# Gate pairs of a two-group trunk layer: the two sums that are rounded first are made directly behind the merges, and the last two merged tiles are split in written order

## The chip, the cores and the metric

The kernel runs on one core of one Trainium2 chip. The metric is the device time of one execution in microseconds (us). The kernel before the change takes 1002.07 us, the median of 3 runs (1001.85 to 1002.22).

## What is computed

One layer of a hybrid backbone is applied to two groups of tokens: a context group of 128 tokens and a denoising group of 512 tokens, 640 tokens together, model width 1024, all in float32. The part that matters here is the gated merge of four token mixers and what stands on both sides of it:

```
    h = rmsnorm(x, lw['norm1_g']) * (1.0 + sc1) + sh1
    mix, kh, vh, s_f, s_b = token_mixers(h, lw, ...)        # ends in the lines below
    x = x + g1 * mix
    h = rmsnorm(x, lw['norm2_g']) * (1.0 + sc2) + sh2
    x = x + g2 * conv_ffn(h, lw['w_up'], ...)
...
    g_a, g_b, g_c, g_d = jnp.split(jax.nn.sigmoid(h @ lw['w_gate'] + lw['b_gate']), N_BRANCH, axis=-1)
    merged = (g_a * (y_a @ lw['w_br_a']) + g_b * (y_b @ lw['w_br_b'])
              + g_c * (y_c @ lw['w_br_c']) + g_d * (y_d @ lw['w_br_d']))
    return merged @ lw['w_o'], kh, vh, s_f, s_b
```

Each of the four gates is a 1024 x 1024 product with `h`, each `w_br_*` a 256 x 1024 product with a mixer's output.

## The kernel before, in words

**Arithmetic.** Every float32 operand of a matmul is split into a high part, rounded by a copy on ScalarE (`oact(..., AF.Copy)`), and a low part, the difference, taken on VectorE (`low`, L1131). A product is three matmuls per 128 rows: high x high, high x low, low x high.

**Gate pairs.** Most of the gate products are done in pairs: output tile n and output tile n+4 of one branch together, by a 2 x 2 block scheme with seven products instead of eight (`gprod`, products 1 to 7, 12 matmuls each; `bprod` does the same for the branch's own weights, 3 matmuls each). There are GPAIR = 14 pairs, (0,2), (0,3) and then four pairs for each of the branches 1, 2 and 3. Pairs 0, 2, 6 and 10 are the first of their branch (`new`). One pair is 105 matmuls.

**What a pair prepares for the next.** For pair n = p+1, pair p makes three weight units from the loaded blocks `r[n]` (names `raw` and `G` in the profile): unit A (`g_a`: high and low of the first block row), unit B (`g_b`: high and low of two sums S0, S1 that `g_sums` makes; they lie in the tile named `D`), and unit C (`g_c`). `g_sums` makes four VectorE additions: S0 and S1 into `D`, then two more in place in `G`/`raw` that unit C and the Z unit (tile `S`) use. A unit's tile is called `w`, every fourth one `B`.

**What a pair computes.** ScalarE and VectorE carry partial results between PSUM banks: `gb` (twice per pair on ScalarE, from bank b1, tile `m`), `ga`, `y`. VectorE then subtracts `gb` from bank b2 (the row `gb<-m,gb`), after which product 3 goes on accumulating in b2: TensorE's product 3 therefore waits for that subtraction. The merges of pair p-1 (`g_merges`, L1213: gate times branch product, added to the merged tiles `MG`) are done in pair p, behind its first product.

**The order of the work.** A scheduler orders each engine's instructions, except those issued through `ovec`, `oact` and `opool` while `fixed[0]` is True: these keep their written order among themselves (`Ordered`, L141 to L151; so they all carry L151). TensorE's order is the scheduler's. `fixed[0]` is set in `g_all` for the pairs.

**Behind the pairs.** `m_split(i)` (L1223) makes high and low of a quarter of the merged tiles, into the tiles `E`, `D`, `B`, `A` for i = 0 to 3. Splits 0 and 1 stand in the last pair; splits 2 and 3 stand behind the merges of the last pair, when `fixed[0]` is False already. `wo_tile` (from L1359, matmuls at L1381) multiplies the merged tiles with w_o in the order E, D, B, A: in its first half all five token blocks accumulate in one bank `m` and four halves of the two banks `g`. VectorE then reads the results out (`wt`, L1391) and adds them to x (L1393). In the last quarter (A) the third and fourth `g` group wait for the first `wt` row that reads a `g` bank. Beside it `up_early` (L1502 to L1547) splits the first weights of the next layer part: loads into `XH` and `XL` (L1508), rounds (L1512), takes the low part (L1513), adds (L1532, L1536) and stores to `upd` (L1519, L1542, L1546). The w_o weights are rounded at L323 and L324. `norm2` (from L1403) normalises each token block and transposes it (L1425).

Of the kernel before, what the change touches and what calls it, by code (L numbers as in the profile page):

```python
# [13 lines left out]
ALU = mybir.AluOpType  # L14
# [56 lines left out]
def tile_step(ctx: ExitStack, tc: tile.TileContext, a: dict, outs: list, dbg=None):  # L71
# [54 lines left out]
    def nm(s):  # L126
        cnt[0] += 1
        return f"{s}_{cnt[0]}"

    def region(tag, shape, dt=F32):  # L130
        return big.tile(shape, dt, tag=tag, name=nm(tag))
# [7 lines left out]
    fixed, boot = [False], [True]  # L139
# [17 lines left out]
    ovec, opool, oact = Ordered(nc.vector), Ordered(nc.gpsimd), Ordered(nc.scalar).activation  # L157
# [802 lines left out]
    for s in SECTIONS:  # L960
        for n in range(2):
            if s in TOK:
                plain(lambda s=s, n=n: rows(a["w_tok"][TOK.index(s), n], 4, 256),
                      lambda w, s=s, n=n: tok_tile(s, n, w))
            else:
                plain(lambda s=s, n=n: feat(a["w_in"][OFF[s] // P + n], dma=s in LOWD),
                      lambda w, s=s, n=n: in_tile(s, n, w))
# [23 lines left out]
    GPAIR = len(PAIRS)  # L991
# [44 lines left out]
    gx, gw = {}, {}  # L1036
# [59 lines left out]
    def y_split():  # L1096
        bi = gx["bi"]
        c, y = gx["C"], R["y" + BR[bi]]
        src = [gx["Y"][:, i * HC:j * HC] for i, j in ((0, 2), (3, 4), (2, 3))]
        dst = [[c[:, h, 0:2].rearrange("p i t -> p (i t)"), c[:, h, 2], y[:, h, 0, HC:T]] for h in range(2)]  # L1100
        for o, x in zip(dst[0][:2], src):
            oact(o, x, AF.Copy)
        lows = [(l, x, h) for h, l, x in zip(dst[0], dst[1], src)]
        return lows[:2], lows[2]
# [26 lines left out]
    def low(w, x, h):  # L1131
        ovec.tensor_tensor(w, x, h.bitcast(F32), ALU.subtract)

    def g_a(p_, r):
        w = gw[p_, "A"] = gunit(p_, 0)
        oact(w[:, 0], r[0], AF.Copy)
        low(w[:, 1], r[0], w[:, 0])

    def g_sums(p_, r):

        s = gw[p_, "S"] = gx["S"] if p_ else region("G", [P, 2, 5, P])
        b21, (b22, b12) = r[0][:, 1], (r[1][:, 0], r[1][:, 1])
        ovec.tensor_tensor(s[:, 0], r[0][:, 0], b12, ALU.add)
        ovec.tensor_tensor(s[:, 1], s[:, 0], b22, ALU.add)
        ovec.tensor_tensor(b12, b12, b22, ALU.add)
        ovec.tensor_tensor(b21, s[:, 1], b21, ALU.add)

    def g_b(p_):
        s = gw[p_, "S"]
        b = gw[p_, "B"] = gunit(p_, 1)  # L1150
        oact(b[:, 0], s, AF.Copy)
        low(b[:, 1], s, b[:, 0])
# [21 lines left out]
    def gprod(o, p_, i, first):  # L1174
        u, n = GPROD[i]
        w = gw[p_, u]
        xh_, xl_ = gx["x"][i]
        for k in range(4):
            for j, (h, x) in enumerate(((0, xh_), (0, xl_), (1, xh_))):
                mm(o, w[:, h, n, k, :], x[:, k, :], start=(first and k == 0 and j == 0),  # L1180
                   stop=(k == 3 and j == 2), skip_group_check=True)
            tick(0.44)
# [9 lines left out]
    def g_merge(p_, i, pb):  # L1192
        bi, n = gp_id(p_)
        n += 4 * i
        gt = gw[p_, "gt", i]
        mg = merged[n // 4][:, n % 4, :]
        ovec.tensor_tensor(c2(gt if bi else mg), pb, c2(gt), ALU.mult)
        if not bi:
            return
        ovec.tensor_tensor(mg, mg, gt, ALU.add)  # L1200

    def g_sig(p_, i, o, x):
        bi, n = gp_id(p_)
        gc = C_BG + GI[BR[bi]] * 8 + n + 4 * i
        oact(o, x, AF.Sigmoid, bias=p1[:, gc:gc + 1])
# [7 lines left out]
    def g_merges(q):  # L1213
        ps, b2, y = gw[q, "ps"], gw[q, "b2"], gw[q, "y"]
        g_merge(q, 0, ps[:, :, 0:HC])
        ovec.tensor_tensor(y[:, 0:HC], b2, y[:, 0:HC], ALU.subtract)
        g_merge(q, 1, c2(y))
        if PAIRS[q] in ((0, 3), (1, 3)):
            n_, t, y = ("yb", "E", ybd) if PAIRS[q][0] == 0 else ("yc", "A", ycd)
            R[n_] = region(t, [P, 2, 2, T], F32R)  # L1220
            pool.dma_start(R[n_], y)

    def m_split(i):  # L1223
        n = 2 * MHN[i]
        w = mh[MHN[i]] = region(MHT[i], [P, 2, 2, T], F32R)
        x = merged[n // 4][:, n % 4:n % 4 + 2, :]
        oact(w[:, 0], x, AF.Copy)
        ovec.tensor_tensor(w[:, 1], x, w[:, 0].bitcast(F32), ALU.subtract)

    def g_pair(p_, r):  # L1230
        n, q = p_ + 1, p_ - 1
        inner, nx = p_ < GPAIR, n < GPAIR
        if not inner:
            g_sig(q, 1, gw[q, "gt", 1], gw[q, "gt", 1])
            g_close(q)
            g_merges(q)
            return
        bi, n0 = gp_id(p_)
        new = n0 == (NPL if bi == 0 else 0)
        if new:  # L1240
            gx["bi"] = bi
        if n0 == (NPL if bi == 0 else 0) + 1 and bi < 3:
            y_load(bi + 1)
        b1, b3 = pm()[:, 0:HC], pm()[:, 0:HC]
        ga = gw[p_, "gt", 0] = gp.tile([P, T], F32, tag="gt", name=nm("ga"))
        gb = gw[p_, "gt", 1] = gp.tile([P, T], F32, tag="gt", name=nm("gb"))
        g_zl(p_, r[p_])
        gprod(b1, p_, 1, True)
        if q >= 0:
            g_sig(q, 1, gw[q, "gt", 1], gw[q, "gt", 1])  # L1250
        oact(b3 if q >= 0 else ga[:, 0:HC], b1, AF.Copy)
        if q >= 0:
            g_close(q)
        ps = gw[p_, "ps"] = pg()
        p1_, p3_ = ps[:, 1, 0:HC], ps[:, 0, 0:HC]
        bprod(p1_, p_, 1, True)
        oact(p3_, p1_, AF.Copy)
        if q >= 0:
            g_merges(q)
        if nx:  # L1260
            g_a(n, r[n])
        lows, x3 = y_split() if new else ([], None)
        gprod(b3, p_, 2, q < 0)
        if q < 0:
            g_split(3, gx["t3"][0])
            ovec.tensor_tensor(ga[:, 0:HC], b3, ga[:, 0:HC], ALU.add)
        g_sig(p_, 0, ga[:, 0:HC], b3 if q >= 0 else ga[:, 0:HC])
        for x in lows:
            low(*x)
        gprod(b1, p_, 6, False)  # L1270
        oact(gb[:, 0:HC], b1, AF.Copy)
        bprod(p3_, p_, 2, False)
        b2 = pm()[:, 0:HC]
        gprod(b2, p_, 5, True)
        if nx:
            g_sums(n, r[n])
            if not new:
                g_b(n)
        gprod(b1, p_, 7, False)
        oact(gb[:, HC:T], b1, AF.Copy)  # L1280
        y = gw[p_, "y"] = gp.tile([P, T], F32, tag="gt", name=nm("y"))
        c2_ = gw[p_, "b2"] = pm()[:, 0:HC]
        bprod(p1_, p_, 6, False)
        oact(y[:, 0:HC], p1_, AF.Copy)
        bprod(c2_, p_, 5, True)
        ovec.tensor_tensor(gb[:, HC:T], b2, gb[:, HC:T], ALU.subtract)
        if new:
            g_b(n)
        if nx:
            late = g_c(n, r[n])  # L1290
            if not new:
                for x in late:
                    low(*x)
            if n + 1 < GPAIR:
                r[n + 1] = gp_load(n + 1)
        else:
            m_split(0)
            m_split(1)
        gprod(b1, p_, 4, False)
        g_sig(p_, 0, ga[:, HC:T], b1)  # L1300
        bprod(p1_, p_, 7, False)
        oact(y[:, HC:T], p1_, AF.Copy)
        if new:
            oact(x3[2], x3[1], AF.Copy)
            low(*x3)
        if nx:
            g_zh(n, r[n])
        gprod(b2, p_, 3, False)
        if n0 == (NPL if bi == 0 else 0) + 1 and bi < 3:
            y_sums()  # L1310
        ovec.tensor_tensor(y[:, HC:T], c2_, y[:, HC:T], ALU.subtract)
        ovec.tensor_tensor(gb[:, 0:HC], b2, gb[:, 0:HC], ALU.subtract)
        if new:
            for x in late:
                low(*x)

    def g_first(r):
        drain(lambda: "ada39" in R)
        g_a(0, r[0])
        g_sums(0, r[0])  # L1320
        g_b(0)
        for x in g_c(0, r[0]):
            low(*x)
        g_zh(0, r[0])
        return r

    def g_all(r):
        drain(lambda: "gx3" in R)
        r[1] = gp_load(1)
        gx["C"] = region("C", [P, 2, 3, HC], F32R)  # L1330
        fixed[0] = True
        sums_ = down_sums()
        for p_ in range(GPAIR + 1):
            for _ in range(4 if p_ else 0):
                next(sums_, None)
            if p_ == GPAIR:
                fixed[0] = False
                for j in range(GATES + 1, GATES + 3):
                    ld[j] = units[j][0]()
                    rd[j] = units[j][1](ld[j])  # L1340
            g_pair(p_, r)
        m_split(2)
        m_split(3)

    PROD = {1: ("A", 0, 2), 2: ("A", 1, 3), 5: ("B", 0, 2), 6: ("B", 1, 3), 7: ("B", 4, 4),
            4: ("C", 0, 2), 3: ("C", 1, 3)}
# [1093 lines left out]
    for i in range(3):  # L2440
        sec, n = SECTIONS[i // 2], i % 2
# [109 lines left out]
```

## Time and profile before

| | |
|---|---|
| median of 3 runs | 1002.07 us (1001.85 to 1002.22) |
| the profiled execution | 1002.13 us |
| its span (first to last instruction) | 1000.4 us |
| granted TensorE clock | 0.998 |
| TensorE busy | 987.6 us (99% of the span) |
| VectorE / ScalarE busy | 861.4 us / 584.5 us |
| gate pairs | 309.7 to 525.3 us of the span |
| first half of w_o | 525.3 to 555 us |

A row of a timeline gives start, duration, engine, line, operation, tile written <- tiles read, shape and count; in brackets the idle time of the engine just before and what ended it. PE is TensorE's matmul, PEld its weight load, DVE VectorE, ACT ScalarE, POOL GpSimd, SPq SyncE's DMA queue. Back to back, the start of one VectorE instruction follows the start of the one before it a little sooner than the printed duration says, so costs in a queue are read from starts. Rows of the chain that ended last give start, duration and what.

### The profile page before, as it was taken

How to read it: one execution, taken by the hardware profiler on the slowest of the kernel's cores; microseconds unless marked ns; L12 is line 12 of the kernel's file. 1: busy time of each engine (PE TensorE's matmuls, PEld its weight loads, DVE VectorE, ACT ScalarE, POOL GpSimd, SP SyncE). 2: the span in 40 equal slices, each digit the busy share in tenths (PEclk: the TensorE clock that was granted, in tenths of full speed). 3: DMA queues.
4: the chain of work that ended last, by engine and by line, in shares of the span. 5: the costliest groups of instructions: out<-in, count | busy, mean ns of one | idle time of the engine just before them, and what ended most of it. 6: DMA issues, size and time to landing. Idle time of an engine off the chain costs nothing.

```text
span 1000.4 us, 18963 instructions
## 1 busy us (share of the span) xinstructions
PE 987.6 (99%) x7467; PEld 936.1 (94%) x7467; DVE 861.4 (86%) x1411; ACT 584.5 (58%) x1009; POOL 170.2 (17%) x227
## 2 busy tenths in 40 slices
PE   8999999999999999999999999999999999999997
PEld 6899999999999999999998799999999999888886
DVE  6678899878677989899879978999999998999796
ACT  6652343445555565555656476777777777756672
POOL 1000020313110223233010021222222222100004
PEclk9999999999999999999999999999999999999999
DMA  9874343498475999899448785766666666976742
GB/s 351 333 255 152 126 139 120 132 254 254 106 216 185 305 240 237 285 252 297 111 159 322 298 317 160 216 160 173 177 168 164 177 170 193 369 259 221 280 127 105
DMA packets 71016, 214.16 MB, mean 214 GB/s; under 512 B 9744, under 2 KB 24880, under 8 KB 68240
## 3 DMA queue, kind: packets, MB, share of 16 engines
q1 hardware_dynamic: 43968, 151.22, 43.1%
q0 software_dynamic: 26960, 61.75, 26.7%
q8 instruction: 58, 0.95, 0.4%
q14 instruction: 30, 0.25, 0.1%
HBM read 168.62 MB, written 48.51 MB: 217 GB/s over the span
## 4 chain that ended last, share of the span: by engine, by line
PE 91%; DVE 3%; DMA 3%; issue 1%; POOL 1%; SPq 0%; ACT 0%; POOLq 0%; ACTq 0%
PE g L1609 21%; PE m L1180 17%; PE g L375 16%; PE m L2081 9%; PE m L1609 5%; PE g L2081 4%; PE g L1189 3%; PE m L1381 3%; PE g L948 2%; PE m L1189 1%; PE m L539 1%; PE m L1604 1%; DMA B<-in_w_ada_dram 1%; DMA S<-in_w_ada_dram 1%; PE g L151 1%
## 5 line engine op out<-in xcount | busy, mean ns | idle before, releaser
L375 PE MATMUL g<-XH,w 128*128 128x320 f32 x704 | 169.4, 316 | 0.0
L375 PEld LDWEIGHTS g<-XH,w 128*128 128x128 f32 x704 | 120.3, 188 | 2.5 <-issue 1.2
L375 PE MATMUL g<-XL,w 128*128 128x320 f32 x352 | 108.7, 309 | 0.0
L1180 PE MATMUL m<-XH,w 128*128 128x320 f32 x336 | 79.8, 309 | 0.0
L375 PEld LDWEIGHTS g<-XL,w 128*128 128x128 f32 x352 | 66.3, 188 | 0.0
L2081 PE MATMUL m<-w,XH 128*128 128x512 f32 x246 | 58.5, 390 | 0.0
L1180 PEld LDWEIGHTS m<-XH,w 128*128 128x128 f32 x336 | 57.6, 188 | 0.0
L2081 PEld LDWEIGHTS m<-w,XH 128*128 128x128 f32 x246 | 46.1, 188 | 9.6
L1180 PE MATMUL m<-XL,w 128*128 128x320 f32 x168 | 51.9, 309 | 0.0
L151 ACT ACTIVATE w<-raw 128x640 fp32r<-128x640 f32 (+3 forms) x53 | 49.6, 952 | 3.2 <-PE g L375 2.0
L151 DVE TENSOR_TENSOR w<-raw,w 128x640 fp32r<-128x640 f32 (+3 forms) x43 | 44.0, 1040 | 2.6 <-ACT w L151 2.6
L151 POOL DMA_DIRECT2D wsum<-in_w_dn_dram x36 | 37.4, 1256 | 43.3 <-issue 39.4
L1180 PE MATMUL m<-X,w 128*128 128x320 f32 x264 | 42.6, 309 | 0.0
L151 DVE SCALAR_TENSOR_TENSOR X<-MG,p2t,X 128x641 f32<-128x641 f32 x44 | 38.9, 884 | 1.0 <-ACT X L151 0.2
L1180 PEld LDWEIGHTS m<-X,w 128*128 128x128 f32 x264 | 39.7, 188 | 0.0
L151 DVE SCALAR_TENSOR_TENSOR X<-X,p2t,X 128x641 f32<-128x641 f32 x44 | 38.9, 884 | 0.9
L1609 PE MATMUL g<-XL,w 128*128 128x320 f32 x240 | 38.7, 310 | 0.0
L1609 PE MATMUL g<-XL,C 128*128 128x320 f32 x240 | 38.3, 309 | 0.0
L1609 PEld LDWEIGHTS g<-XL,w 128*128 128x128 f32 x240 | 36.0, 188 | 0.6 <-ACT MG L151 0.3
L1609 PEld LDWEIGHTS g<-XL,C 128*128 128x128 f32 x240 | 36.0, 188 | 0.0
L1180 PEld LDWEIGHTS m<-XL,w 128*128 128x128 f32 x168 | 31.5, 188 | 0.0
L336 ACT ACTIVATE w<-raw 128x1024 fp32r<-128x1024 f32 (+1 forms) x22 | 24.3, 1102 | 12.3 <-PE m L948 8.2
(612 smaller groups left out, 2840.8 us busy)
## 6 DMA issues: line engine op xcount, KB each, us to landing
wsum<-in_w_dn_dram POOLq DMA_DIRECT2D x30, 512.0 KB, 11.0
raw<-in_w_up_dram SPq DMA_DIRECT2D x30, 512.0 KB, 5.2
raw<-in_w_gp_dram SPq DMA_DIRECT2D x21, 640.0 KB, 5.8
raw<-in_w_in_dram SPq DMA_DIRECT2D x19, 512.0 KB, 4.2
H<-in_w_adt_dram SPq DMA_DIRECT2D x19, 512.0 KB, 4.0
raw<-wsum SPq DMA_DIRECT2D x12, 512.0 KB, 5.5
actx<-X POOLq DMA_DIRECT2D x22, 256.0 KB, 4.8
wsum<-wsum POOLq DMA_DIRECT2D x10, 512.0 KB, 10.6
```

What stands on the lines that cost most here:

```text
L151: r = f(*args, **kw)
L336: high = lambda: act(w[:, 0], raw, AF.Copy)
L375: mm(o, w[:, h, k0 + k, :], r(k)[:, s], start=(k == 0 and i == 0), stop=(k == kt - 1 and i == 2))
L539: mm(m[W * g:W * g + W, (i - s0) * W:(i - s0 + 1) * W], lhs, rhs, start=True, stop=True, tile_position=(64 * par, W * g))
L948: mm(o, x(kx)[:, ts], w[:, h, k, :], start=(kx == 0 and i == 0), stop=(kx == 7 and i == 2))
L1180: mm(o, w[:, h, n, k, :], x[:, k, :], start=(first and k == 0 and j == 0), stop=(k == 3 and j == 2), skip_group_check=True)
L1189: mm(o, w[:, h, n, 4, :], x[l], start=(first and j == 0), stop=(j == 2), skip_group_check=True)
L1381: mm(m, mh[MHN[q]][:, hx, k % 2, t * P:(t + 1) * P], wo[q][:, hw, k % 2, :], start=(k == 0 and i == 0), stop=(k == 7 and i == 2))
L1604: mm(o, w[:, k, :], x[:, k, :], start=(first and not part and k == 0 and j == 0), stop=(part == 1 and k == 3), skip_group_check=True)
L1609: z = mm(o, w[:, k, :], x[:, k, :], start=(first and k == 0 and j == 0), stop=(k == 3 and j == 2), skip_group_check=True)
L2081: mm(ps, s[t // 4][:, hx, k, o:o + P], w[:, hw, k, c0:c1], start=first, stop=i == 2 and bi == len(batch) - 1 and k == len(ks) - 1, skip_gr ...
```

## The change

`g_a` is cut in two: `g_a` (the rounding on ScalarE) stays at its place and `g_al` (the low part on VectorE) is issued later. `g_sums` is cut in two: `g_s01` (S0 and S1) is issued directly behind the merges, in pair 0 behind the first addition to `ga`; `g_s23` (the other two) and `g_al` follow behind the first sigmoid and, in a `new` pair, the low parts of `y_split`. `g_b` is issued at one place for all pairs, behind product 5; in `new` pairs it was two products later. At the end, `m_split(2)` is called inside the merges of the last pair, behind the first of its two merges, and `fixed[0]` stays True until `m_split(3)`.

```diff
     def g_a(p_, r):
         w = gw[p_, "A"] = gunit(p_, 0)
         oact(w[:, 0], r[0], AF.Copy)
+
+    def g_al(p_, r):
+        w = gw[p_, "A"]
         low(w[:, 1], r[0], w[:, 0])
 
-    def g_sums(p_, r):
+    def g_s01(p_, r):
 
         s = gw[p_, "S"] = gx["S"] if p_ else region("G", [P, 2, 5, P])
+        ovec.tensor_tensor(s[:, 0], r[0][:, 0], r[1][:, 1], ALU.add)
+        ovec.tensor_tensor(s[:, 1], s[:, 0], r[1][:, 0], ALU.add)
+
+    def g_s23(p_, r):
+        s = gw[p_, "S"]
         b21, (b22, b12) = r[0][:, 1], (r[1][:, 0], r[1][:, 1])
-        ovec.tensor_tensor(s[:, 0], r[0][:, 0], b12, ALU.add)
-        ovec.tensor_tensor(s[:, 1], s[:, 0], b22, ALU.add)
         ovec.tensor_tensor(b12, b12, b22, ALU.add)
         ovec.tensor_tensor(b21, s[:, 1], b21, ALU.add)
 
@@ g_merges
         g_merge(q, 0, ps[:, :, 0:HC])
+        if q == GPAIR - 1:
+            m_split(2)
         ovec.tensor_tensor(y[:, 0:HC], b2, y[:, 0:HC], ALU.subtract)
@@ g_pair
             g_merges(q)
         if nx:
             g_a(n, r[n])
+            if q >= 0:
+                g_s01(n, r[n])
         lows, x3 = y_split() if new else ([], None)
         gprod(b3, p_, 2, q < 0)
         if q < 0:
             g_split(3, gx["t3"][0])
             ovec.tensor_tensor(ga[:, 0:HC], b3, ga[:, 0:HC], ALU.add)
+            g_s01(n, r[n])
         g_sig(p_, 0, ga[:, 0:HC], b3 if q >= 0 else ga[:, 0:HC])
         for x in lows:
             low(*x)
+        if nx:
+            g_al(n, r[n])
+            g_s23(n, r[n])
         gprod(b1, p_, 6, False)
         oact(gb[:, 0:HC], b1, AF.Copy)
         bprod(p3_, p_, 2, False)
         b2 = pm()[:, 0:HC]
         gprod(b2, p_, 5, True)
         if nx:
-            g_sums(n, r[n])
-            if not new:
-                g_b(n)
+            g_b(n)
         gprod(b1, p_, 7, False)
...
         ovec.tensor_tensor(gb[:, HC:T], b2, gb[:, HC:T], ALU.subtract)
-        if new:
-            g_b(n)
         if nx:
             late = g_c(n, r[n])
@@ g_all
             if p_ == GPAIR:
-                fixed[0] = False
                 for j in range(GATES + 1, GATES + 3):
                     ld[j] = units[j][0]()
                     rd[j] = units[j][1](ld[j])
             g_pair(p_, r)
-        m_split(2)
         m_split(3)
+        fixed[0] = False
```

**Where instructions move, 1: VectorE in pair 6, the first pair of branch 2.** `MG` is the last merge of pair 5, `w_4834` the low part of unit A, `C` the low parts of `y_split`, `D<-raw,G` S0 and `D<-D,G` S1, `w_4910` (after: `w_4887`) the low part of unit B, and `gb_4800<-m_...` the subtraction from b2. Before:

```order
L151 TENSOR_TENSOR MG_354_3769<-MG_354_3769,gb_4645 128x640
L151 TENSOR_TENSOR w_4834<-raw_4757,w_4834 128x1280
L151 TENSOR_TENSOR C_3853<-D_2872,C_3853 128x640
L151 TENSOR_TENSOR C_3853<-D_2872,C_3853 128x320
L151 TENSOR_TENSOR D_2872<-raw_4757,G_4758 128x640
L151 TENSOR_TENSOR D_2872<-D_2872,G_4758 128x640
L151 TENSOR_TENSOR G_4758<-G_4758 128x640
L151 TENSOR_TENSOR raw_4757<-D_2872,raw_4757 128x640
L151 TENSOR_TENSOR gb_4800<-m_4870,gb_4800 128x320
L151 TENSOR_TENSOR w_4910<-D_2872,w_4910 128x1280
```

And after:

```order
L151 TENSOR_TENSOR MG_354_3769<-MG_354_3769,gb_4645 128x640
L151 TENSOR_TENSOR D_2872<-raw_4757,G_4758 128x640
L151 TENSOR_TENSOR D_2872<-D_2872,G_4758 128x640
L151 TENSOR_TENSOR C_3853<-D_2872,C_3853 128x640
L151 TENSOR_TENSOR C_3853<-D_2872,C_3853 128x320
L151 TENSOR_TENSOR w_4834<-raw_4757,w_4834 128x1280
L151 TENSOR_TENSOR G_4758<-G_4758 128x640
L151 TENSOR_TENSOR raw_4757<-D_2872,raw_4757 128x640
L151 TENSOR_TENSOR w_4887<-D_2872,w_4887 128x1280
L151 TENSOR_TENSOR gb_4800<-m_4874,gb_4800 128x320
```

The two sums into `D` have moved ahead of the low parts of `C` and of unit A, and the low part of unit B ahead of the subtraction `gb`. On ScalarE the rounding of unit B has moved ahead of the second `gb` copy in the `new` pairs. In the other pairs only the two `D` rows and the low part of unit A have changed places.

**Where instructions move, 2: VectorE behind the last pair.** `ga`, `y`, `gb` and the two `MG` rows are the merges of pair 13, `B` and `A` the low parts of splits 2 and 3, the `w` rows the low parts of w_o weights, and the rows `XL_561<-XH` , `C_6143<-XL`, `MG_565<-XH` and `S_568<-XH` those of `up_early` (L1513, after the change L1524). Before:

```order
L151 TENSOR_TENSOR ga_5896<-g_5919,ga_5896 128x640
L151 TENSOR_TENSOR y_5984<-m_5985,y_5984 128x320
L151 TENSOR_TENSOR MG_337_3586<-MG_337_3586,ga_5896 128x640
L151 TENSOR_TENSOR gb_5897<-y_5984,gb_5897 128x640
L324 TENSOR_TENSOR w_6061<-raw_6059,w_6061 128x1024
L151 TENSOR_TENSOR MG_354_3769<-MG_354_3769,gb_5897 128x640
L151 TENSOR_TENSOR B_6053<-MG_337_3586,B_6053 128x1280
L151 TENSOR_TENSOR A_6056<-MG_354_3769,A_6056 128x1280
L1513 TENSOR_TENSOR XL_561_6119<-XH_6087,XL_561_6119 128x1024
L324 TENSOR_TENSOR w_6123<-raw_6064,w_6123 128x1024
L1513 TENSOR_TENSOR C_6143<-XL_559_6088,C_6143 128x1024
L1513 TENSOR_TENSOR MG_565_6162<-XH_6087,MG_565_6162 128x1024
```

And after:

```order
L151 TENSOR_TENSOR ga_5896<-g_5919,ga_5896 128x640
L324 TENSOR_TENSOR w_6061<-raw_6059,w_6061 128x1024
L151 TENSOR_TENSOR MG_337_3586<-MG_337_3586,ga_5896 128x640
L1524 TENSOR_TENSOR XL_561_6119<-XH_6087,XL_561_6119 128x1024
L1524 TENSOR_TENSOR C_6143<-XL_559_6088,C_6143 128x1024
L151 TENSOR_TENSOR B_6050<-MG_337_3586,B_6050 128x1280
L151 TENSOR_TENSOR y_5984<-m_5985,y_5984 128x320
L324 TENSOR_TENSOR w_6123<-raw_6064,w_6123 128x1024
L151 TENSOR_TENSOR gb_5897<-y_5984,gb_5897 128x640
L324 TENSOR_TENSOR w_6165<-raw_6066,w_6165 128x1024
L151 TENSOR_TENSOR MG_354_3769<-MG_354_3769,gb_5897 128x640
L1524 TENSOR_TENSOR S_568_6185<-XH_6087,S_568_6185 128x1024
```

The rows `XL_561` and `C_6143` of `up_early`, which were behind both splits, now stand ahead of split 2; `y`, `gb` and the second `MG` row stand behind split 2, with w_o and `up_early` rows between them. Split 3 (`A`) follows two rows further down.

On TensorE the only moves are in pairs 3, 7 and 11, where two matmuls of the next pair's product 1 stood ahead of product 4 and now stand at their own place, and behind pairs 3 and 7, where three matmuls of a product 5 did the same. On SyncE's queue the store of `XL_561` to `upd` moves ahead of one w_o load, and the first load of the next part's weights (L1470) ahead of a reload of `XH` and of two stores to `upd`. GpSimd's queue is unchanged.

More of the change, by code (lines that the diff above doesn't have):

```diff
@@ L1319, in g_first @@
         g_a(0, r[0])
-        g_sums(0, r[0])
+        g_al(0, r[0])
+        g_s01(0, r[0])
+        g_s23(0, r[0])
         g_b(0)
```

## The prediction

> **What bounds the kernel now.** I read the page first, then the stages, then TensorE's waits, and last the timeline around each wait. The page's first line, and the table of busy time by stage (start:end, length, then PE, PEld, DVE, ACT, POOL, the granted clock, the DMA share and GB/s), here the gate pairs and the first half of w_o:
>
> ```profile
> span 1000.4 us, 18963 instructions
> ```
>
> ```profile
> 309.70:525.30 215.60, 215.60 (x1469) 215.07 (x1468) 186.69 (x251) 125.94 (x208) 47.15 (x54) 1.00 0.85 228
> 525.30:555.00 29.70, 28.51 (x127) 23.25 (x127) 28.15 (x35) 15.09 (x16) 0.00 (x0) 1.00 0.87 335
> ```
>
> TensorE is the bound: in the gate pairs it does 1469 matmuls in 215.6 us, 0.147 us each, almost without a break, and its work is the same after the change. What the change can take away is only the time that TensorE waits in these stages. The view of waits has two such rows in the code around the change:
>
> ```profile
> PEld m L1180 <- ACT gb L151: 0.5, 3, 0.2
> ```
>
> ```profile
> PE g L1381 <- DVE wt L1391: 1.2, 1, 1.2
> ```
>
> So there are three small waits in the pairs and one in the first half of w_o. The chain shows the first of the three:
>
> ```profile
> 366.50 2.24 PE m L1180 x14
> ```
>
> 14 matmuls should take 14 x 0.147 = 2.06 us, so 0.18 us are lost, and three times that is the 0.5 us of the row of waits. In w_o the break stands behind these rows of TensorE:
>
> ```profile
> 539.36 1.52 PE L1381 MATMUL m<-w,B 128*128 128x512 f32 x6
> ```
>
> ```profile
> 546.15 1.52 PE L1381 MATMUL m<-w,A 128*128 128x512 f32 x6
> ```
>
> ```profile
> 550.24 0.84 PE L1381 MATMUL m<-w,E 128*128 128x512 f32 x3
> 552.27 3.06 PE L1381 MATMUL g<-w,A 128*128 128x512 f32 x12 [1.19 <-DVE wt L1391]
> ```
>
> A quarter of the first half is 30 such matmuls (five token blocks of six), and takes 546.15 - 539.36 = 6.79 us, 0.226 us each. The three at 550.24 end at 550.92, and the next begin at 552.27: 1.35 us lost.
>
> All that the change could win is therefore 0.5 + 1.35 = 1.9 us of 1002. A measurement of this kernel can tell 0.2%, 2.0 us, from no change; below I use that bound.
>
> **Part 1: the sums S0 and S1 ahead of the low part of unit A.** The waits at 366, 428 and 490 us (pairs 3, 7, 11) are the end of one queue: VectorE makes the low part of A, then S0 and S1; ScalarE rounds S (unit B) only then, and its `gb` copy, for which TensorE waits, stands behind that:
>
> ```profile
> 361.88 1.49 DVE L151 TENSOR_TENSOR w<-raw,w 128x1280 fp32r<-128x1280 f32 x1
> ...
> 364.14 0.83 DVE L151 TENSOR_TENSOR D<-D,raw 128x640 f32<-128x640 f32 x1
> ```
>
> ```profile
> 365.06 1.28 ACT L151 ACTIVATE w<-D 128x1280 fp32r<-128x1280 f32 x1 [2.92 <-DVE D L151]
> 366.24 0.42 ACT L151 ACTIVATE gb<-m 128x320 f32<-128x320 f32 x1
> ```
>
> ```profile
> 366.71 0.19 PEld L1180 LDWEIGHTS m<-XH,B 128*128 128x128 f32 x1 [0.18 <-ACT gb L151]
> ```
>
> With S0 and S1 first, S1 is ready the length of the low part earlier: 365.06 becomes about 363.65 (the low part takes 1.41 us of the queue, from 361.88 to 363.29 by the next row's start). ScalarE had 2.92 us idle before it, so unit B is rounded by 364.9 and `gb` waits only for TensorE. The three waits go: -0.5 us. What is late next there is the bank itself, which ScalarE copies in time in all other pairs (no row of waits). The low part of A, moved behind the sums, is first needed when pair n begins, several us later: nothing.
>
> The sums now wait for both loaded blocks where the low part waited for one. A block is loaded about one pair ahead:
>
> ```profile
> 358.21 0.33 SPq L1122 DMA_DIRECT2D G<-in_w_gp_dram  x1
> ```
>
> is the one that pair 4 adds, and S0 of pair 4 stands 15 us behind that of pair 3 (363.29). So I cost this at nothing; if a load were late, the low part and unit B would wait with it.
>
> **Part 2: unit B at one place in `new` pairs.** Here something is added to a path that had slack. In pairs 2, 6 and 10 the low part of unit B now stands ahead of the subtraction `gb<-m,gb`, and TensorE's product 3 waits for that subtraction. Pair 6 before:
>
> ```profile
> 407.48 1.49 DVE L151 TENSOR_TENSOR w<-raw,w 128x1280 fp32r<-128x1280 f32 x1
> ...
> 413.09 0.49 DVE L151 TENSOR_TENSOR gb<-m,gb 128x320 f32<-128x320 f32 x1
> ```
>
> ```profile
> 412.05 0.44 ACT L151 ACTIVATE gb<-m 128x320 f32<-128x320 f32 x1 [3.52 <-PE m L1180]
> ```
>
> ```profile
> 414.93 0.31 PE L1180 MATMUL m<-XH,w 128*128 128x320 f32 x1
> ```
>
> From 407.48 to 413.09 VectorE does seven rows back to back. After the change the same seven come first, then the low part of B, 1.40 us of the queue: `gb` runs from 414.50 to 414.99. Product 3 would begin at 414.93 (its matmul; the weight load some 0.15 us earlier). In part 1 the weight load went on 0.05 us behind the copy it waited for, which gives a start at 415.04 for the load and a loss between 0.1 and 0.25 us; I take 0.2. Pair 10 has the same rows 61.78 us later, so twice: +0.4 us. Pair 2 has two merge rows fewer ahead of it (branch 0 only writes `MG`), which leaves it over 1.5 us: nothing. Bounds: 0 (if those rows close up a little) and 2 x 0.5. ScalarE's rounding of B ahead of the second `gb` copy falls into the 3.52 us that it waited there: nothing.
>
> **Part 3: splits 2 and 3 in written order.** What should be won is the wait at 552.27. It is the end of a VectorE queue without a break from 533.08 on:
>
> ```profile
> 527.01 0.82 DVE L151 TENSOR_TENSOR ga<-g,ga 128x640 f32<-128x640 f32 x1
> 527.74 0.48 DVE L151 TENSOR_TENSOR y<-m,y 128x320 f32<-128x320 f32 x1
> 528.14 0.82 DVE L151 TENSOR_TENSOR MG<-MG,ga 128x640 f32<-128x640 f32 x1
> 528.87 0.82 DVE L151 TENSOR_TENSOR gb<-y,gb 128x640 f32<-128x640 f32 x1
> 529.61 1.22 DVE L324 TENSOR_TENSOR w<-raw,w 128x1024 fp32r<-128x1024 f32 x1
> 530.74 0.82 DVE L151 TENSOR_TENSOR MG<-MG,gb 128x640 f32<-128x640 f32 x1
> 533.08 1.49 DVE L151 TENSOR_TENSOR B<-MG,B 128x1280 fp32r<-128x1280 f32 x1 [1.52 <-ACT B L151]
> ...
> 549.19 0.69 DVE L1391 TENSOR_TENSOR wt<-m,F 128x512 f32<-128x512 f32 x1
> ```
>
> ```profile
> 530.83 1.06 ACT L1512 ACTIVATE XL<-XH 128x1024 fp32r<-128x1024 f32 x1 [0.21 <-DMA XH<-in_w_up_dram]
> 531.79 1.26 ACT L151 ACTIVATE B<-MG 128x1280 fp32r<-128x1280 f32 x1
> ```
>
> ```profile
> 525.03 0.80 SPq L1508 DMA_DIRECT2D XH<-in_w_up_dram  x2
> ```
>
> VectorE idles 1.52 us before split 2, because ScalarE, in the order of its queue, first waits for the `XH` load and rounds it. Splitting earlier would fill that hole. But in the order after the change ScalarE still rounds `XL<-XH` ahead of split 2, and VectorE has the row `XL_561<-XH` ahead of its split, and `y`, `gb` and the second `MG` behind. So VectorE does `ga`, the w_o row and one `MG` row, is done by about 529.7 (527.01 + 0.73 + 1.13 + 0.75 by the starts above), and then waits for ScalarE's rounding: 530.83 + 1.06 + 0.03 = 531.92. The idle time is 2.2 us instead of 1.52. From there it has the 16.11 us of rows that stood between 533.08 and 549.19, plus `y`, `gb` and the second `MG`: 0.40 + 0.74 + 0.75 = 1.89 us by the starts above (0.75 for a row of the same width as `gb`, 0.74, with a little for its own wait). I went through these rows in the new order, and none waits again; the nearest is `MG_565`, whose rounding on ScalarE waits for split 3 and ends just as VectorE gets there. So `wt` starts at 531.92 + 16.11 + 1.89 = 549.92 instead of 549.19. TensorE resumes as far behind `wt` as before: +0.73 us, a wait of 2.1 us.
>
> By the same count split 2 is done at 535.6 (behind two rows of 1.14 us: 531.92 + 2.28 + 1.40) and split 3 at 542.9; TensorE reads them in its third and fourth quarter, from 539.36 and 546.15 on, so both are covered by over 3 us; without that cover each us would count in full. The reorderings on SyncE's queue move a 512 KB load ahead of stores that `up_early` waits for later. They can reach TensorE only through `norm2`, whose first transposes follow VectorE's row closely:
>
> ```profile
> 567.52 0.75 DVE L1413 TENSOR_SCALAR C<-X,st 128x1024 f32<-128x1024 f32 x1 [0.47 <-POOL st L318]
> 568.76 1.03 PE L1425 MATMUL m<-cst,C 128*128 128x128 f32 x8
> ```
>
> The slack is 568.76 - 568.27 = 0.5 us, so I cost it at nothing, with up to 0.5 us against me. GpSimd's queue is as before.
>
> Bounds of part 3: if `XH` landed so early that nothing waited, `wt` would come by 547.8 and the wait would go (-1.35); if the load takes the median of the loads of its line,
>
> ```profile
> DMA to landing us min/median/max: 5.8/6.8/9.4
> ```
>
> 6.8 us instead of its own 5.8, it is +1.7.
>
> **The sum.** -0.5 + 0.4 + 0.7 = +0.6 us. The profiled execution took 1002.13 us (span 1000.4 us), 0.06 above the median of 1002.07, so I forecast 1002.13 + 0.6 - 0.06 = 1002.7 us.
>
> **The rivals.**
>
> *The split fills the hole (chance 0.14).* If VectorE does not wait for `XH`, the 552 wait goes: -0.5 + 0.4 - 1.35 gives 1000.6 us. For it: the idle 1.52 us is there to be filled. Against it: the load landed 5.8 us behind its issue, at 530.83, and that issue itself waits for the last gate product. Without the losses of part 2 it would be 1000.2, still within 0.2%.
>
> *The wait moves on to `norm2` (0.12).* If the stores to `upd`, now behind a load, hold ScalarE's next rounding of `XL` and VectorE with it by 1 us, the 0.5 us of slack at the first transposes is used up and another 0.5 us lost: 1003.2 us.
>
> *VectorE stands still behind `XL<-XH` (0.09), the slower side.* Everything behind that row now waits for one load, which before had 4 us of slack on VectorE (its row came behind both splits, 533.08 + 2 x 1.40 = 535.9). Each us that `XH` lands later than 530.83 costs one. From 1.4 us on (landing over 7.2 us behind issue, between the median and the longest of its line) the kernel is slower by over 0.2%; at 2 us it takes 1004.7 us.
>
> *A long wait slows the clock (0.02).* The end of the trace shows what a long idle time does. TensorE's last matmul ends at 993.27 (in the first of these two rows), and the granted clock is 1.00 until 997 and about half behind it:
>
> ```profile
> 993.00:994.00 1.00, 0.27 (x3) 0.10 (x1) 0.97 (x3) 0.46 (x1) 0.00 (x0) 1.00 0.00 0
> ...
> 997.00:998.00 1.00, 0.00 (x0) 0.00 (x0) 0.00 (x0) 0.00 (x0) 0.00 (x0) 0.54 0.97 389
> ```
>
> So a wait of some 3.8 us would also slow the matmuls behind it; if the clock came back after as long, half of 3.8 us is another 1.9. It needs `XH` 1.7 us late on top of my 2.1 us: 1002.7 + 1.7 + 1.9 = 1006.3 us. The wait before was 1.35 us with the clock at 1.00, so it is unlikely. The Trainium skill ("TensorE: Matmul & The Clock Gate", section on the HAM clock gate) has this as a rule: after an idle window of about 3.4 us TensorE falls to half its clock, and a busy window of the same length releases it. The trace agrees with 3.8 us for the fall; by the page's figure the rival would begin 0.4 us earlier and cost 0.2 us less.
>
> *The change does nothing visible:* with 0.6 us forecast, this cannot be told from it.
>
> **How the numbers follow.** The forecast has 0.60, the rest (unnamed, 0.03) is split evenly. Faster by over 0.2% (under 1000.1) needs both waits gone and more: 0.03. Slower (over 1004.1): 0.09 + 0.02 + 0.01 = 0.12 at most, with a part of the XH rival under the bound: 0.11. The same: 0.86. The range reaches from the first rival's 1000.6 to 1004.0, where the slower rival begins; it leaves out about 0.15.
>
> **What the changed profile would show.** Right: no wait of a gate product for `gb` on ScalarE in pairs 3, 7, 11; two short waits of product 3 for `gb` on VectorE near 415 and 476.5; VectorE idle about 2.2 us before `XL<-XH`; `wt` near 549.9 and TensorE's wait there near 2.1 us. Wrong: if that wait is shorter than 1.35 us, part 3 fails; if one above 1 us turns up elsewhere, the sum does.

## The result, and the profile after

The changed kernel takes 1004.83 us (median of 8 runs, 1004.02 to 1006.56) against 1002.14 us for the kernel before in the same series: the ratio is 1.0026, with a 95% interval of 1.0015 to 1.0037 (1.5 to 3.7 us). It is slower by 2.7 us, where 0.6 us was forecast. One execution of the kernel before took 1615.92 us; all ratios leave out such slow executions, and the profiled one of `e5_split_first` (1377.63 us, clock 0.654) was one of them. The profiled execution took 1005.34 us with a span of 1003.6 us and a mean granted clock of 0.996.

The two small parts came out as written. In the changed kernel's waits of the weight loads (waited for: us in total, times, longest) there is no row any more of a gate product that waits for `gb` on ScalarE, and this one is new:

```profile
PEld m L1186 <- DVE gb L151: 0.4, 2, 0.2
```

That is the three waits of part 1 gone, and two waits of 0.2 us for product 3. Lines behind the change have moved down: L1381 is now L1392, L1391 is L1402, L1513 is L1524.

The ending, on VectorE:

```profile
528.08 0.82 DVE L151 TENSOR_TENSOR MG<-MG,ga 128x640 f32<-128x640 f32 x1
531.08 1.23 DVE L1524 TENSOR_TENSOR XL<-XH,XL 128x1024 fp32r<-128x1024 f32 x1 [2.18 <-ACT XL L1523]
...
549.08 0.69 DVE L1402 TENSOR_TENSOR wt<-m,F 128x512 f32<-128x512 f32 x1
```

VectorE idles for 2.18 us, where 2.2 was forecast. `wt` starts at 549.08 instead of 549.92, but this whole trace runs 0.85 us ahead (below), so the forecast holds. And on TensorE:

```profile
545.29 1.52 PE L1392 MATMUL m<-w,A 128*128 128x512 f32 x6
...
549.37 0.84 PE L1392 MATMUL m<-w,E 128*128 128x512 f32 x3
552.15 4.60 PE L1392 MATMUL g<-w,A 128*128 128x512 f32 x12 [1.94 <-DVE wt L1402]
556.59 0.84 PE L1392 MATMUL m<-w,E 128*128 128x512 f32 x3
```

The three matmuls end at 550.05 and the next start at 552.15: TensorE is idle for 2.10 us, as forecast. But then comes what the sum did not have. The twelve matmuls behind the wait take 556.59 - 552.15 = 4.44 us; in the kernel before they took 555.16 - 552.27 = 2.89 us. The stages of 1 us show why (the third column from the right is the granted clock):

```profile
552.00:553.00 1.00, 0.85 (x3) 0.69 (x4) 1.00 (x3) 0.00 (x0) 0.00 (x0) 0.73 0.89 379
553.00:554.00 1.00, 1.00 (x4) 0.81 (x3) 0.90 (x2) 0.00 (x0) 0.00 (x0) 0.50 1.11 471
554.00:555.00 1.00, 1.00 (x3) 0.78 (x3) 0.12 (x1) 0.00 (x0) 0.00 (x0) 0.50 1.04 430
555.00:556.00 1.00, 1.00 (x4) 0.76 (x3) 0.97 (x2) 0.00 (x0) 0.00 (x0) 0.57 1.12 358
556.00:557.00 1.00, 1.00 (x6) 0.84 (x5) 0.51 (x2) 0.21 (x1) 0.00 (x0) 1.00 0.69 272
```

The clock is halved. It lacks 0.27 + 0.50 + 0.50 + 0.43 = 1.70 us of full speed, so it was at half for 3.4 us, from 552.46 (1.00 less 0.27/0.50 of a microsecond) to 555.86.

Setting the starts of the same matmuls of both traces side by side shows where the time goes. TensorE reaches the pairs 0.85 us earlier than in the trace of before (it is 0.82 ahead at 33 us already, by its waits for the first loads; no code there was changed). At 520 us it is 0.87 ahead, behind the w_o wait (`m<-w,E` at 556.59 against 555.16) it is 1.43 late: the ending costs 2.30 us, 0.75 in the wait and 1.55 in the clock. Two small waits follow, which the trace of before does not have:

```profile
650.38 2.04 PE L1620 MATMUL g<-XL,C 128*128 128x320 f32 x12 [0.34 <-DVE X L151]
```

```profile
918.63 0.28 PE L304 MATMUL g<-cst,gcol 128*16 128x128 f32 x1 [0.25 <-DVE gcol L291]
```

By the starts they cost 0.63 and 0.42 us. With them the changed kernel is 2.47 us late at 918 us, and its last store lands 0.7 us later still.

### The profile page after: what moved, and what is told of

Same layout as the page of the kernel before. It is cut to its first block, busy times and chain, and to the rows that moved or that the text cites. A ratio compares the mean times of both kernels' runs of the same rounds, so it can differ in the third digit from the quotient of the medians.

```text
span 1003.6 us, 18966 instructions
## 1 busy us (share of the span) xinstructions
PE 989.3 (99%) x7467; PEld 936.8 (93%) x7467; DVE 861.4 (86%) x1411; ACT 586.7 (58%) x1009; POOL 170.1 (17%) x227
## 4 chain that ended last, share of the span: by engine, by line
PE 91%; DVE 4%; DMA 2%; issue 1%; POOL 1%; ACT 0%; SPq 0%; POOLq 0%; DVEq 0%
PE g L1620 21%; PE m L1186 17%; PE g L375 16%; PE m L2092 8%; PE m L1620 5%; PE g L2092 4%; PE g L1195 3%; PE m L1392 3%; PE g L948 2%; PE m L151 2%; PE g L151 1%; PE m L1195 1%; PE m L539 1%; PE m L1615 1%; DMA A<-in_w_ada_dram 1%
## 5 line engine op out<-in xcount | busy, mean ns | idle before, releaser
L151 ACT ACTIVATE gb<-m 128x320 f32<-128x320 f32 x28 | 12.3, 438 | 38.4 <-PE m L1186 38.4
```

What stands on the lines that cost most here:

```text
L151: r = f(*args, **kw)
```

## The experiments

**The theory:** the ending makes TensorE's w_o wait longer, and from about 2 us on such a wait halves the clock for 3.4 us. **The rivals:** the pairs' new order, or transfers moved by it, cost part of the 2.7 us; or the half clock has another cause than the length of the idle time.

### Which half of the change

`e1_pairs` has parts 1 and 2 alone:

```diff
         g_merge(q, 0, ps[:, :, 0:HC])
-        if q == GPAIR - 1:
-            m_split(2)
...
             if p_ == GPAIR:
+                fixed[0] = False
...
+        m_split(2)
         m_split(3)
-        fixed[0] = False
```

> Parts 1 and 2 alone: the pairs as in the changed kernel, the ending (splits 2 and 3) as before. Theory (the loss is the w_o wait and the half clock behind it): the wait there is 1.35 us again, the clock stays at 1.00, and the time is that of before - 0.5 + 0.4 = 1002.0 us (1001.6 to 1002.5). Rival (the pairs' new order, or transfers that it shifts, make part of the 2.7 us): 1003 us or more with the clock at 1.00 in w_o.

Measured: 1002.39 us, ratio to before 0.9997 (0.9988 to 1.0006). `e2_ending` is the opposite, the pairs of before with `m_split(2)` inside the merges and `fixed[0]` True until `m_split(3)`:

> Part 3 alone: the pairs as before, splits 2 and 3 in written order. Theory: wait of 2.1 us and a stretch of half clock of about 3.4 us behind it, 1002.1 + 0.75 + 1.55 = 1004.4 us (1003.8 to 1005). Rival (the 2.7 us need the pairs' order too): 1002.9 us, the wait alone.

Measured: 1004.63 us, ratio 1.0022 (1.0012 to 1.0032). So the ending makes the loss, and the pairs none that the interval (0.9 us to either side) can show. Yet the single traces held two surprises. They are of executions off the median: `e1_pairs` took 1004.31 us in its own, `e2_ending` 1003.39. First TensorE in `e1_pairs`, with the old ending, and one stage of its clock:

```profile
549.57 0.84 PE L1391 MATMUL m<-w,E 128*128 128x512 f32 x3
552.83 4.28 PE L1391 MATMUL g<-w,A 128*128 128x512 f32 x12 [2.42 <-DVE wt L1401]
```

```profile
555.00:556.00 1.00, 1.00 (x3) 0.77 (x3) 0.96 (x2) 0.00 (x0) 0.00 (x0) 0.50 1.00 297
```

and in `e2_ending`:

```profile
549.66 0.84 PE L1382 MATMUL m<-w,E 128*128 128x512 f32 x3
552.86 3.01 PE L1382 MATMUL g<-w,A 128*128 128x512 f32 x12 [2.35 <-DVE wt L1392]
```

```profile
555.00:556.00 1.00, 1.00 (x6) 0.81 (x5) 0.96 (x3) 0.09 (x1) 0.00 (x0) 1.00 1.06 430
```

The old ending waited 2.58 us here, not 1.35, and lost its clock too (4.07 us to the next start); the new one waited 2.52 us and kept it (2.85 us to the next start). So the wait varies from run to run whichever the ending, and a wait of 2.5 us does not always halve the clock. The length comes from two loads that land one behind the other. ScalarE in the kernel before:

```profile
529.55 1.06 ACT L1512 ACTIVATE C<-XL 128x1024 fp32r<-128x1024 f32 x1 [1.77 <-DMA XL<-in_w_up_dram]
```

in `e1_pairs`:

```profile
530.11 1.06 ACT L1522 ACTIVATE C<-XL 128x1024 fp32r<-128x1024 f32 x1 [3.00 <-DMA XL<-in_w_up_dram]
531.38 1.06 ACT L1522 ACTIVATE XL<-XH 128x1024 fp32r<-128x1024 f32 x1 [0.21 <-DMA XH<-in_w_up_dram]
```

and in the changed kernel:

```profile
528.71 1.06 ACT L1523 ACTIVATE C<-XL 128x1024 fp32r<-128x1024 f32 x1 [1.80 <-DMA XL<-in_w_up_dram]
529.99 1.06 ACT L1523 ACTIVATE XL<-XH 128x1024 fp32r<-128x1024 f32 x1 [0.22 <-DMA XH<-in_w_up_dram]
```

`C<-XL` waits for the XL load and `XL<-XH` for the XH load, and the second row starts 1.27 or 1.28 us behind the first in all eight traces that have them in this order. That distance is the loads' own: in `e6_v2` (below), where ScalarE comes to these rows late and waits for neither, XL is issued at 523.25 us and lands 7.1 us later, XH at 525.60 and 6.0 us later, again 1.3 us apart. So the landing of XL tells that of XH too. Six of the eight traces, two of which come below, give one rule (the other two, whose waits are edited, have 20.36 us in the fourth column as well):

| trace | ending | XL issue to `C<-XL` | `C<-XL` to `wt` | TensorE idle | clock behind |
|---|---|---|---|---|---|
| before | old | 6.87 us | 19.64 us | 1.35 us | 1.00 |
| `e1_pairs` | old | 8.09 | 19.64 | 2.58 | half |
| `e7_longer_idle` | old | 7.73 | 19.65 | 2.90 (0.68 added) | half |
| after | new | 6.89 | 20.37 | 2.10 | half |
| `e8_after_again` | new | 7.21 | 20.36 | 2.42 | half |
| `e2_ending` | new | 7.31 | 20.36 | 2.52 | 1.00 |

(XL issue is the row of SyncE's queue, `wt` the row of VectorE that reads the bank `m`.) From the landing of XL to `wt` the new ending takes 0.72 us more in these traces; the rest is how long the loads take: 1.35 + (8.09 - 6.87) = 2.57 us against 2.58 measured in `e1_pairs`.

### Is it the idle time

`e4_after_warm` puts small matmuls of zeros into the wait of the changed kernel:

```diff
         for t in range(5):
             m = pm() if nh == 1 else wo["acc"][t]
+            if (nh, kk_, t) == (0, 3, 3):
+                for _ in range(48):
+                    mm(wo["acc"][0][0:64, 0:64], warm, warm, start=True, stop=True)
```

> The changed kernel, with 48 tiny matmuls of zeros into the bank that has just been read out, put into the w_o wait (they are extra work, and the three matmuls that stood in front of the wait now stand behind it). The wait for wt stays, but TensorE is idle in it for under 1 us. Theory: the clock stays at 1.00 and the twelve matmuls behind the wait take 2.9 us instead of 4.4: 1004.8 - 1.55 + 0.68 for the three displaced matmuls = 1003.9 us. Rival (the half clock has nothing to do with the idle time): half clock as before this edit, 1004.8 + 0.68 = 1005.5 us.

```profile
546.85 2.88 PE L1395 MATMUL g<-w,A 128*128 128x512 f32 x12
550.09 1.68 PE L1391 MATMUL m<-warm 128*64 128x64 bf16 x48 [0.36 <-DVE wt L1405]
552.43 3.01 PE L1395 MATMUL g<-w,A 128*128 128x512 f32 x12 [0.66 <-DVE wt L1405]
```

Measured: 1004.11 us, ratio 1.0017 (1.0008 to 1.0025). TensorE resumes as late as ever, but the twelve matmuls take 2.85 us to the next start (`m<-w,E` at 555.28): with the wait covered, the clock stays. `e7_longer_idle` goes the other way on the kernel before, and lengthens the idle time without touching VectorE or a queue:

```diff
-                        mm(m, ...)
+                        z = mm(m, ...)
+                        if nh == 0:
+                            wo["last"] = z
+                        elif t == 0:
+                            tc.add_manual_dep(z.ins, wo["last"].ins.name, ...)
```

> The kernel before, all as it was on VectorE, ScalarE and the queues, with one change on TensorE: the three matmuls m<-w,E that stand in front of the w_o wait stand behind it. The wait ends when it did, but TensorE is idle in it for 2.03 us instead of 1.35. Theory (the clock falls when an idle time gets near 2 us): the three displaced matmuls cost 0.68, and the twelve behind the wait run at half clock in most runs, 1.5 us more: 1002.2 + 0.68 + 1 to 1.5 = 1003.9 to 1004.4 us. Rival (the half clock comes from the changed order of loads and splits, not from the length of the idle time): 1002.9 us with the clock at 1.00.

```profile
546.89 2.88 PE L1381 MATMUL g<-w,A 128*128 128x512 f32 x12
552.51 4.50 PE L1381 MATMUL g<-w,A 128*128 128x512 f32 x12 [2.74 <-DVE wt L1396]
```

Measured: 1004.28 us, ratio 1.0021 (1.0012 to 1.0030), with single runs from 1002.3 to 1006.4. The clock in its stages:

```profile
552.00:553.00 1.00, 0.49 (x1) 0.49 (x2) 1.00 (x3) 0.00 (x0) 0.00 (x0) 0.65 1.05 440
...
555.00:556.00 1.00, 1.00 (x5) 0.76 (x4) 0.52 (x1) 0.00 (x0) 0.00 (x0) 0.64 0.90 260
```

with 0.50 between: 0.35 + 0.50 + 0.50 + 0.36 = 1.71 us lacking, again 3.4 us at half. The loads were late in this trace, so 2.22 of its 2.90 us would have been there without the edit; what the edit does is read from the times. Of the 2.3 us that it costs (the kernel before has 1002.00 us in this series), 0.68 are the three matmuls behind the wait, and the other 1.6 us are about the price of the half clock. Nothing of the change is in this kernel, so the half clock does not need the changed order.

`e8_after_again` is the changed kernel itself:

> The changed kernel once more, unedited, for a second trace and eleven more times. Theory: 1004.8 us; a wait of 2 to 2.6 us, its length following the landing of the XH load, and half clock for 3.4 us behind it unless the idle time is cut in two by the clock's own window. Rival (the first trace was an odd one): no half clock near 552 and a time below 1003.5 us.

Measured: 1004.29 us, the median of ten executions, ratio 1.0021 (1.0013 to 1.0030). Five of the ten took 1002.64 to 1003.82 us and five 1004.75 to 1005.99. That fits half clock in some executions and not in others, as in the traces, though only one of the ten was traced, at 1005.28 us.

```profile
549.55 0.84 PE L1392 MATMUL m<-w,E 128*128 128x512 f32 x3
552.65 4.43 PE L1392 MATMUL g<-w,A 128*128 128x512 f32 x12 [2.25 <-DVE wt L1402]
```

```profile
553.00:554.00 1.00, 1.00 (x6) 0.82 (x5) 1.00 (x3) 0.00 (x0) 0.00 (x0) 0.96 0.95 399
...
557.00:558.00 1.00, 1.00 (x5) 0.79 (x4) 0.85 (x2) 0.88 (x1) 0.00 (x0) 0.84 0.98 389
```

Half clock again for 3.4 us (0.04 + 3 x 0.50 + 0.16 = 1.70 lacking), but here it begins at 553.92, 1.27 us after TensorE went on; in the first trace it began 0.31 us after, in `e7_longer_idle` 0.2 us before.

### Taking the wait away

`e3_after_free` lets TensorE go on without `wt`: in the first half the matmuls of all five blocks are written ahead of the read-out.

```diff
-            v = 0 if t < 4 else 1
...
+            ms.append((t, m))
+            if nh == 0 and t < 4:
+                continue
+            for t, m in ms:
+                v = 0 if t < 4 else 1
```

> The changed kernel, with the read-out of the first four w_o accumulators written behind the matmuls of all five: the third and fourth group no longer wait for the first row that reads a g bank. Theory: no wait of TensorE near 552, the clock stays at 1.00 in w_o, 1004.8 - 2.1 - 1.55 = 1001.2 us (1000.8 to 1001.8). Rival (1.5 us or more of the loss is elsewhere, in later transfers): only the 2.1 us go, 1002.7 us.

```profile
546.82 5.60 PE L1393 MATMUL g<-w,A 128*128 128x512 f32 x24
...
557.61 1.42 PE L1393 MATMUL m<-w,A 128*128 128x512 f32 x5 [0.66 <-DVE w L324]
...
568.84 1.09 PE L1442 MATMUL m<-cst,C 128*128 128x128 f32 x8 [0.50 <-DVE st L317]
```

Measured: 1003.06 us, ratio 1.0005 (0.9996 to 1.0014). The wait and the half clock are gone (24 matmuls without a break), and with them about 2 us of the changed kernel's loss (the ratio was 1.0026), not 3.65: a w_o weight and the first transposes are now late, since VectorE is. Part of the wait only moved on.

`e5_split_first` works at the cause: what waits for the loads stays behind split 3.

```diff
+        def behind(ins, key):
+            tc.add_manual_dep(ins.ins, wo[key].ins.name, ...)
+        def late(hi, lo, v):
+            behind(act(hi, v, AF.Copy), "act")
+            behind(vec.tensor_tensor(lo, v, hi.bitcast(F32), ALU.subtract), "vec")
...
-            part(flat(w[:, 0:2]), flat(w[:, 2:4]), r)
+            late(flat(w[:, 0:2]), flat(w[:, 2:4]), r)
```

Here `wo["act"]` and `wo["vec"]` are the last split's two instructions, and the first three additions of `up_early` go behind them too.

> The changed kernel, with the rows of up_early that wait for the XH and XL loads (the roundings on ScalarE, the low parts and the first sums on VectorE) kept behind split 3. Split 2 no longer stands behind a load. Theory: VectorE idles about 1.5 us instead of 2.2, two rows move behind the read-out, the wt row that TensorE waits for comes about 2 us earlier, the wait is under 0.3 us and the clock stays at 1.00: 1004.8 - 2.0 - 1.55 = 1001.2 us; up to 0.9 us more if a later w_o weight (w, L324) now comes late: 1001.2 to 1002.1. Rival (the loss lies in the order of the merges and splits, not in the load): 1004 us or more.

Measured: 1003.26 us, ratio 1.0008 (0.9999 to 1.0017): no longer slower, but above the range expected. A second series of the same kernel is to show why:

> The changed kernel with only the XH rows kept behind split 3, once more, for a trace that can be read (it took 1003.3 us where 1001.2 to 1002.1 was expected). Theory: no wait for the wt row and no half clock, but a wait of about 1 us or more for a w_o weight whose low part now stands behind the read-out rows on VectorE. Rival: the wait for wt is there as in the changed kernel, with half clock behind it.

Measured: 1002.64 us, ratio 0.9999 (0.9990 to 1.0008). VectorE and TensorE in it:

```profile
530.34 1.49 DVE L151 TENSOR_TENSOR B<-MG,B 128x1280 fp32r<-128x1280 f32 x1 [1.34 <-ACT B L151]
...
534.36 1.23 DVE L324 TENSOR_TENSOR w<-raw,w 128x1024 fp32r<-128x1024 f32 x1 [1.27 <-ACT w L323]
```

```profile
550.84 1.66 PE L1392 MATMUL g<-w,A 128*128 128x512 f32 x6 [0.98 <-DVE wt L1402]
```

Both expectations missed: the wait for `wt` is there, but it is 1.15 us long (549.69 to 550.84), and the clock stays. VectorE still idles twice, since split 2, standing ahead of the second merge, waits for its own rounding, and a w_o row behind it for another.

`e6_v2` keeps that and puts split 2 behind both merges:

```diff
         g_merge(q, 0, ps[:, :, 0:HC])
-        if q == GPAIR - 1:
-            m_split(2)
...
+        m_split(2)
         m_split(3)
         fixed[0] = False
```

> As the run before it, with split 2 moved back behind both merges (in written order merges, split 2, split 3, then the rows that wait for the XH load); the pairs as in the changed kernel. By the rows of the changed kernel's trace VectorE then has no idle time there: split 2 at 530.7, split 3 at 532.1, XL<-XH at 533.5, and the wt rows ready before TensorE needs them. Theory: no wait near 552, clock 1.00, the time of before - 1.35 - 0.1 = 1000.8 us (1000.4 to 1001.3): faster than both. Rival (something else than the wait and the clock costs time at the ending): not under 1002 us.

Measured: 1000.00 us (999.73 to 1000.96), ratio 0.9977 (0.9968 to 0.9986): faster than both kernels.

```profile
531.63 0.83 DVE L151 TENSOR_TENSOR MG<-MG,gb 128x640 f32<-128x640 f32 x1
532.37 1.49 DVE L151 TENSOR_TENSOR B<-MG,B 128x1280 fp32r<-128x1280 f32 x1
533.80 1.49 DVE L151 TENSOR_TENSOR A<-MG,A 128x1280 fp32r<-128x1280 f32 x1
535.21 1.22 DVE L1531 TENSOR_TENSOR XL<-XH,XL 128x1024 fp32r<-128x1024 f32 x1
```

```profile
550.81 1.07 PE L1391 MATMUL m<-w,E 128*128 128x512 f32 x4
551.71 2.88 PE L1391 MATMUL g<-w,A 128*128 128x512 f32 x12
554.43 0.62 PE L1391 MATMUL m<-w,E 128*128 128x512 f32 x2
```

VectorE has no idle time at the splits, and TensorE no break. Two variants finish it. `e11_old_pairs_v2` has this ending on the pairs of before:

> The same ending (merges, split 2, split 3, then the rows that wait for the XH load) on the pairs of the kernel before. Theory: the ending is worth all of it, the pairs - 0.1 us: the three waits for gb (0.5 us) are back, the two of product 3 (0.4) are gone: 1000.1 us. Rival (the pairs' new order is worth more in every run than its waits show): 1000.6 us or more.

Measured: 1000.39 us, between the two times expected, ratio 0.9980 (0.9970 to 0.9989), with the old row for `gb` back in the waits of its weight loads, and two others:

```profile
PEld g L1619 <- DVE X L151: 0.9, 1, 0.9
PEld m L1180 <- ACT gb L151: 0.5, 3, 0.2
PEld g L304 <- DVE gcol L291: 0.5, 1, 0.5
```

`e9_v2_late_b` is `e6_v2` with unit B in `new` pairs where it was before the change:

```diff
-        if nx:
+        if nx and not new:
             g_b(n)
...
         ovec.tensor_tensor(gb[:, HC:T], b2, gb[:, HC:T], ALU.subtract)
+        if new:
+            g_b(n)
```

> The version with the merges first and both splits ahead of the rows that wait for the XH load (1000.0 us), with unit B in the new pairs back where it was before the change (two products later). Theory: the two waits of product 3 of 0.2 us each in pairs 6 and 10 go, nothing takes their place: 1000.0 - 0.4 = 999.6 us. Rival (another row in those pairs is late then): 1000.0 us or more.

Measured: 999.57 us (999.12 to 1000.46), ratio 0.9967 (0.9956 to 0.9979), and its waits have no row for `gb` at all. It has the lowest median of all. The intervals of the last three overlap, so the 0.4 us from one to the next agree with the rows of waits, but are not settled by the times.

## Why the prediction was wrong

- **Part 1 (-0.5) and part 2 (+0.4): right** by their rows of waits. The time of `e1_pairs`, at 0.9997, agrees, but cannot resolve 0.1 us.
- **Part 3 (+0.73 in the wait): right in mechanism and size.** The table has 0.72 us at equal landing of the loads. The reading of 530.83 as the landing of XH was right as well: issued at 525.03, it lands 5.8 us later.
- **The clock: this step failed.** The rival "a long wait slows the clock" had the right mechanism and nearly the right price (1.9 us; 1.55 measured), but the prediction let it decide only from 3.8 us of idle time, and gave it 0.02. That threshold was read from one fall at the end of the trace, and by the reading in the last section 0.4 us of its 3.8 are only the place of the last matmul in a window of the clock. The runs show falls behind 2.10, 2.42, 2.58 and 2.90 us, and none behind 1.15 and 1.35 (nor, in one trace, behind 2.52). So the sum lacked 1.55 us, which by itself leads from 1002.7 to 1004.3 us; the 0.5 us from there to the median lie within the interval.
- **The base of the sum.** "The wait before was 1.35 us" held for one execution, whose XL load took 6.87 us to `C<-XL`, the shortest of the six (up to 8.09). An execution at the median of the total need not be at the median of the stage. At 7.3 us, by the table's rule, the old ending waits 1.8 us and the new 2.5. This would also explain why `e6_v2`, which ends the dependence on the loads, gains 2 us and not the 1.35 + 0.1 expected.
- **The rivals.** The split did not fill the hole in the changed order, as argued; `e6_v2` shows the order in which it does. "VectorE stands still behind `XL<-XH`" was right that each microsecond of a late load counts, but it does so in both endings. The 4 us of slack that it gave the old one were not there, since ScalarE rounds XH ahead of split 2 in both: in `e1_pairs` the loads take 1.22 us longer than in the kernel before, and the wait is 1.23 us longer.
- **Open:** the two small waits at 650 and 918 us, and the 0.7 us of the last store. `e11_old_pairs_v2` has such waits for `X` (0.9 us) and `gcol` (0.5 us) too, without the changed ending, so they are not bound to it; whether the change makes them more frequent was not tried.

## What to carry to other kernels

A forced order is only as good as what the rows in front of it wait for: before moving a step earlier, put the rows that wait for a load behind it, or the scheduler may place them ahead. Where a queue ends in a wait for a load, take the landing time from several executions, since one trace can show the shortest. And price a TensorE wait with the clock: behind 2.10 us of idle time the twelve matmuls cost another 1.55 us here.

## What the runs showed of the hardware

Half clock lasted 3.4 us in each of four traces, whatever work was done, and began 0.2 us before, or 0.3, 1.3 and 1.5 us after TensorE went on. So the moment is not set by the end of the wait. The Trainium skill ("TensorE: Matmul & The Clock Gate", Part 1 on the HAM clock gate) has a free-running activity window of 3413 ns; the traces agree with its length. It also puts the fall behind at least one idle window; here the traces differ, since 2.10 us were enough.

The traces also show a fixed step. From the fall near 552 us to the one behind the last matmul it is 447.15 us in the changed kernel (552.46 to 999.60) and in `e7_longer_idle`, and 443.73 us in `e1_pairs` and `e8_after_again`: 131 and 130 times 3.413 us, the length that the clock's record in these traces gives for each stretch of half clock. So the ends of the windows can be counted back from the last fall in a trace that has no other.

A reading that fits all these traces, though no run was made to test it: the clock is set at the end of each such window by the busy share within it. In the 3.41 us ahead of the falls TensorE was idle for 2.10 us in the changed kernel (549.05 to 552.46), 2.14 in its second trace, 2.69 in `e7_longer_idle` and 1.92 in `e1_pairs` (half clock from 554.32). Without a fall, the wait of the kernel before puts 1.35 us into one window. In `e2_ending` a window ends at 551.38 (131 steps ahead of its last fall, at 998.53), and cuts the 2.52 us into 1.04 and 1.48. The limit would lie between 1.48 and 1.92 us of idle time in a window. By the same count the 3.8 us that the prediction read at the end of the first trace are one wholly idle window (993.66 to 997.08) and the 0.4 us ahead of it, from the last matmul at 993.27.
